# Layer 1's gate product on float16 weight parts in a diffusion transformer kernel on Trainium2

## The chip, the cores and the metric

One core of one Trainium2 chip runs the whole program in one launch. The metric is the time of one execution in microseconds on the device. A core has TensorE (PE: matrix products into PSUM; its weight loads are listed apart as PEld), VectorE (DVE), ScalarE (ACT), GpSimd (POOL) and SyncE (SP), each with its own queue of instructions that it runs in order, and 16 DMA engines that serve the queues on which transfers are issued. Here SyncE and GpSimd issue nearly all of the loads.

## The reference, cut to what matters

Two layers of a diffusion transformer on 256 tokens and 256 context rows of width 2048. Each layer modulates its normalized input with a shift, a scale and a gate that come from a product of the condition with `ada_w`; layer 0 mixes with a Fourier branch, layer 1 with windowed attention, and both multiply the branch's output by `silu(z)`, where z is a part of the product of h with the layer's input weights.

```python
def _attention_branch(h, hc, w_in, sink, rows, cols, need_ctx):
    ...
    q, k, v, z = jnp.split(h @ w_in, [D_BRANCH, D_BRANCH + kvw, D_BRANCH + 2 * kvw], axis=-1)
    ...
    y = jnp.moveaxis(o, 0, 1).reshape(b, n, D_BRANCH) * jax.nn.silu(z)
...
def reference(x, c, ctx, c_ctx, norm_g, ada_w, ada_b, w_out, ...):
    for i in range(DEPTH):
        ...
        shift, scale, gate = jnp.split((jax.nn.silu(c) @ ada_w[i] + ada_b[i])[:, None, :], 3, axis=-1)
        h = _rmsnorm(x, norm_g[i]) * (1 + scale) + shift
        ...
        x = x + gate * (y @ w_out[i])
    return _rmsnorm(x, final_g)
```

In layer 1, z has 4096 columns for the 256 tokens only, so its weights are 2048 x 4096 float32, 32 MB.

## The kernel before, in words

**Accuracy by parts.** A float32 operand is kept as a high and a low part, and a product is the sum of three products (high by high, high by low, low by high): `mm3`, lines 145 to 147. Two kinds of parts occur. In the float32 kind (`half_split`, lines 66 and 67) ScalarE rounds 1024 columns of a weight tile to the high part `wh`, and VectorE subtracts to get the low part `wl`. In the float16 kind (`split16`, lines 137 and 138) both parts `wf` are float16, and the weights are first multiplied by a power of two `up` that keeps them in float16's span. That power comes from the sum of the squares of all the weights, so those must have been read once before; the inverse power is multiplied in later. Layer 0's gate product and output product are of the float16 kind.

**The stages that the change touches** follow each other in time:

- *Output product of layer 0* (658 to about 1002 us): 32 steps `i`, in two halves of 16; a step takes one 1 MB weight tile `wo0` through SyncE's queue into one of three `raw` buffers (line 50), splits it into two `wf` in one of six `ws` buffers each, and does 48 products of 512 columns. Beside it run three other loads of work. `scan_loads` (line 824, GpSimd's queue) brings pieces of 512 columns of weights that are needed later, and `scan_sums` (line 817) squares and sums them on ScalarE a step later; this goes on for steps 0 to 13 only. `xT`, the layer's input, is loaded on GpSimd's queue in steps 12 to 15 and 28 to 31. And jobs of `ada_jobs` bring the modulation's weights `adw` of layer 0's gate and of layer 1: a job is one tile of 2048 columns, and its dot products with the condition's row `cb` run on VectorE (line 796; one or two per half of 1024 columns). `ada_rate` says how many jobs a step has, where nothing is listed one. Ahead of this stage such a job comes as two halves, `zr` on SyncE's queue (two buffers) and `wa` on GpSimd's (from the six `ws` buffers); within the stage it comes whole on SyncE's queue into a `raw` buffer (`out0[0]` is true there).
- *Transition* (to about 1004 us): row sums and the normalization of layer 1's input.
- *Key stage* (about 1004 to 1092 us): the modulated rows are made as float32 parts, for the tokens `h1` (tiles `hx1`; named h in the profile) and for the context `h1c`, and the key and value product runs over eight tiles `wkv`, split by lines 66 and 67. Then PSUM is emptied by ScalarE (`S.copy` and `Abs`, lines 1135, 1136 and 1142), a product sums the absolute values for the scale of v (line 1147), and attention begins.
- *Attention* (1092 to about 1632 us): a list of units (`units`) is emitted between the stages of softmax, two units to a stage (`filler`): 64 units of the q product (float32 parts), 32 blocks of the z product with two units each, and 12 units `o` of the output product. A z unit (lines 1320 to 1326) does for each of eight ranks k of 128 rows one product of `wh` with the whole 512-column tile `hx1[k]`, high and low part of h side by side, and one of `wl` with its first 256 columns. After the block's second unit the two halves of PSUM are added (lines 1330 and 1331), then comes z's tanh (1332) and its product (1333). `stage_s` makes scores, softmax and its float16 parts `f` (lines 1377 and 1378), which SyncE turns by DMA into `ft`; `stage_o` (lines 1395 and 1396) multiplies them with v in float16 products of 256 columns. `d_turn` (line 1209) prepares `dsc`, the factor that undoes the scale of v when the branch's output is multiplied by z's part.

The order of the instructions on each engine is made by a scheduler from the order in which they are written; `tc.issue_after(x)` ties what is written under it behind x.

Of the kernel before, what the change touches and what calls it, by code (L numbers as in the profile page):

```python
# [10 lines left out]
F32 = mybir.dt.float32  # L11
# [6 lines left out]
P = 128  # L18
# [14 lines left out]
def tile_dit(ctx: ExitStack, tc: tile.TileContext, a: dict, out: bass.AP):  # L33
# [591 lines left out]
    def h_bound():  # L625
        m = adap.tile([P, 2], F32, name="hm")
        V.tensor_reduce(m[:, 0:1], gs0.rearrange("p k s -> p (k s)"), axis=AX.X, op=ALU.max, apply_absolute_value=True)
        V.tensor_reduce(m[:, 1:2], sh0.rearrange("p k s -> p (k s)"), axis=AX.X, op=ALU.max, apply_absolute_value=True)
        V.scalar_tensor_tensor(m[:, 0:1], m[:, 0:1], 46.0, m[:, 1:2], op0=ALU.mult, op1=ALU.add)
        return as_b(m[:, 0:1])  # L630
# [8 lines left out]
    for g in range(G):  # L639
# [6 lines left out]
        if g == 13:  # L646
            with tc.issue_after(evacs[g - 2][1]), tc.issue_after(evacs[g - 2][0]):
                hb = h_bound()
                n4 = as_b(nrm[:, 30:38])
# [119 lines left out]
    def ada_jobs():  # L769
        for pieces in ((0,), (1, 2, 3)):  # L770
            for kh in range(2):
# [9 lines left out]
                if True:  # L781
                    for i, fg in order:
                        for f in range(2):
                            q = slice(f * 1024, f * 1024 + 1024)
                            if f == 0 and not out0[0]:
                                wf = adat.tile([P, 1024], F32, tag="zr", name="zr", bufs=2)
                                nc.sync.dma_start(wf, a["adw"][i, kh, fg][:, q])
                            elif not out0[0]:
                                wf = wsp.tile([P, 1024], F32, tag="ws", name="wa")
                                nc.gpsimd.dma_start(wf, a["adw"][i, kh, fg][:, q])  # L790
                            else:
                                if f == 0:
                                    w = raw(a["adw"][i, kh, fg])
                                wf = w[:, q]
# [17 lines left out]
    scans, pend = iter(range(64)), []  # L812

    def scan_sums():
        while pend:
            t, j = pend.pop(0)
            S.activation(t, t, AF.Square, accum_out=scn[:, j : j + 1])

    def scan_loads(n):
        for j in [next(scans) for _ in range(n)]:  # L820
            for q in range(2):
# [3 lines left out]
                pend.append((t, j * 2 + q - 64 * (j >= 40)))  # L825
# [20 lines left out]
    with tc.tile_pool(name="yp", reuse_waits="tile", bufs=32) as ypool:  # L846
# [142 lines left out]
        ada_rate = {**{i: 2 for i in (*range(6, 10), *range(17, 25))}, **{i: 0 for i in (14, 15, 16, 29, 30, 31)}}  # L989
        for i in range(32):  # L990
# [5 lines left out]
            if sw == 0:  # L996
                with tc.issue_after(last_cast[0]):
                    scan_sums()
                scan_loads({6: 1, 7: 1, 8: 1, 9: 1}.get(i, 2) if i < 14 else 0)
# [8 lines left out]
            elif i == 31:  # L1008
# [24 lines left out]

    x1d = dram.tile([2, P, D], F32, name="x1d")
# [57 lines left out]
    with tc.tile_pool(name="h1", reuse_waits="tile", bufs=16) as h1p:  # L1092
# [4 lines left out]
        with tc.tile_pool(name="kvp", reuse_waits="tile", bufs=2) as kvp:  # L1097
            hc1 = []
            oner = kvp.tile([P, P], F32R, name="oner", bufs=1)
            S.activation(oner, ident, AF.Identity, bias=1.0, scale=0.0)  # L1100
            for k in range(KT):
# [16 lines left out]
                hc1.append(hc)  # L1118
            o = [[psum() for _ in range(2)] for _ in range(4)]
            for kg in range(8):  # L1120
                with tc.issue_after(h_end[0]), tc.issue_after(sq_end[0]):
                    w = ws_split(raw(a["wkv"][kg])) if kg else [w0, half_split(wr, 1)]
                for j in range(2):
                    k = kg * 2 + j
                    wh, wl = w[j]
                    for tb in range(4):
                        h = (hx1, hc1)[tb // 2][k]
                        c = (tb % 2) * P
                        for kv in range(2):
                            q = slice(kv * 512, (kv + 1) * 512)  # L1130
                            mm3(o[tb][kv], h[:, c : c + P], h[:, N + c : N + c + P], wh[:, q], wl[:, q], k == 0, k == KT - 1)
            kr = []
# [36 lines left out]
        with tc.tile_pool(name="at", reuse_waits="tile", bufs=2) as at:  # L1169
# [35 lines left out]
            def d_turn(half):  # L1205
# [3 lines left out]
                V.tensor_copy(dsc[:, half * 4 : half * 4 + 4], o[:, 0::P])  # L1209
# [65 lines left out]
            def prep(u):  # L1275
# [6 lines left out]
                return half_split(raws1[src], i % 2)  # L1282

            ready = {}

            def emit_unit():
# [30 lines left out]
                else:  # L1317
                    if i == 0:
                        o.append(psum())
                    for k in range(i * 8, i * 8 + 8):  # L1320
                        q = slice((k % 8) * P, (k % 8 + 1) * P)
                        for part in (0, 1) if k < KT - 1 else (1, 0):
                            if part == 0:
                                PE.matmul(o[0], wh[:, q], hx1[k], start=k == 0, stop=k == KT - 1)  # L1324
                            else:
                                PE.matmul(o[0][:, 0:N], wl[:, q], hx1[k][:, 0:N], start=False, stop=False)  # L1326
                    if i == 1:
                        th = at.tile([P, N], F32, tag="th", name="th", bufs=3)
                        zs = at.tile([P, N], F32, tag="zs", name="zs", bufs=1)
                        S.copy(zs, o[0][:, N : 2 * N])  # L1330
                        V.tensor_tensor(zs, o[0][:, 0:N], zs, op=ALU.add)
                        S.activation(th, zs, AF.Tanh, scale=0.5)
                        V.scalar_tensor_tensor(th, th, 1.0, zs, op0=ALU.add, op1=ALU.mult)
# [326 lines left out]
```

## Time and profile before

| | us |
|---|---|
| three runs | 1776.87, 1776.41, 1772.83 |
| median | 1776.41 |
| profiled execution, its time | 1775.4 |
| its span, first to last instruction | 1773.6 |

The profile is of one execution. Its page gives for each engine the busy time, the share of the span and the number of instructions (26403 in all). The chain that ended last is followed back from the last instruction. A group of instructions is one line of the program on one engine with its tiles (output<-inputs) and shapes; behind the count stand the busy time in us, the mean of one in ns, and the idle time of the engine just before them with what ended it. A row of DMA issues has the tile, the queue, the count, the size and the median time from issue to landing in us.

### The profile page before, as it was taken

To read this page: it belongs to the slowest core of one execution; us is meant where nothing else is said; L and a number is where in the kernel's file an instruction comes from. 1 tells how busy PE (TensorE), PEld (TensorE's weight loads), DVE (VectorE), ACT (ScalarE), POOL (GpSimd) and SP (SyncE) were. 2 spreads that over 40 slices of the span, in tenths; PEclk is the share of its full clock that TensorE was granted. 3 is DMA by queue.
4 is the path that set the end of the run, shared out by engine and by line. 5 is a ranking of instruction groups with operands and counts; after the bars stand their busy time and mean duration, and the time that the engine had idled before them with its cause. 6 is when DMAs were issued, how large, how long until landed. Compare 5 with 4: busy or idle time off the path is not lost.

```text
span 1773.6 us, 26403 instructions
## 1 busy us (share of the span) xinstructions
PE 1738.5 (98%) x9517; PEld 1221.7 (69%) x9517; DVE 1393.7 (79%) x2401; ACT 1060.4 (60%) x1989; POOL 294.8 (17%) x368
## 2 busy tenths in 40 slices
PE   6999999999999999999999999999999999999997
PEld 4679999644444444446444888788888888887886
DVE  5779888797777788876885744899999999996455
ACT  5545556477777745553122534787888888885343
POOL 0002111212222132000000000412302230233010
PEclk9999999999999999999999999999999999999999
DMA  9998999778998889865775323588888888887543
GB/s 393 417 346 252 282 264 262 291 285 318 329 306 316 314 293 349 324 249 181 288 297 187 120 95 119 166 207 200 223 205 211 214 214 211 208 212 248 191 166 143
DMA packets 220962, 438.74 MB, mean 247 GB/s; under 512 B 154720, under 2 KB 155120, under 8 KB 189088
## 3 DMA queue, kind: packets, MB, share of 16 engines
q1 hardware_dynamic: 182784, 351.85, 60.6%
q0 software_dynamic: 33904, 78.25, 14.8%
q10 hardware_dynamic: 4144, 6.95, 1.2%
q8 instruction: 75, 1.23, 0.3%
q14 instruction: 55, 0.45, 0.1%
HBM read 391.91 MB, written 12.59 MB: 228 GB/s over the span
## 4 chain that ended last, share of the span: by engine, by line
PE 90%; DVE 4%; DMA 3%; ACT 2%; issue 1%; POOL 0%; ACTq 0%; POOLq 0%; SPq 0%; DVEq 0%
PE ps L145 24%; PE ps L147 24%; PE ps L146 24%; PE ps L1324 6%; PE ps L1326 3%; PE ps L1395 1%; PE ps L1360 1%; PE ps L1361 1%; PE ps L1396 1%; DMA ft<-f 1%; PE ps L286 1%; DMA raw<-in_awp 1%; DVE wl L67 1%; ACT act L864 0%; ACT wf L137 0%
## 5 line engine op out<-in xcount | busy, mean ns | idle before, releaser
L67 DVE TENSOR_TENSOR wl<-raw,wh 128x1024 fp32r<-128x1024 f32 x213 | 281.1, 1324 | 145.5 <-ACT wh L66 129.2
L66 ACT CAST wh<-raw 128x1024 fp32r<-128x1024 f32 x213 | 222.4, 1045 | 178.4 <-PE ps L146 149.7
L146 PE MATMUL ps<-act,wf 128*128 128x512 f16 x512 | 194.0, 379 | 0.0
L147 PE MATMUL ps<-act,wf 128*128 128x512 f16 x512 | 191.1, 379 | 0.0
L145 PE MATMUL ps<-act,wf 128*128 128x512 f16 x512 | 189.8, 379 | 0.6 <-ACT wf L137 0.3
L1324 PE MATMUL ps<-h,wh 128*128 128x512 f32 x512 | 184.8, 396 | 0.0
L147 PEld LDWEIGHTS <-wf 128*128 128x128 f16 x960 | 93.9, 98 | 113.3
L145 PEld LDWEIGHTS <-wf 128*128 128x128 f16 x960 | 93.7, 98 | 113.4 <-ACT wf L137 4.3
L145 PE MATMUL ps<-y,wf 128*128 128x512 f16 x448 | 169.5, 379 | 0.9 <-ACT wf L137 0.9
L146 PE MATMUL ps<-y,wf 128*128 128x512 f16 x448 | 169.8, 379 | 0.0
L146 PEld LDWEIGHTS <-wf 128*128 128x128 f16 x960 | 93.9, 98 | 109.0
L147 PE MATMUL ps<-y,wf 128*128 128x512 f16 x448 | 165.6, 379 | 0.0
L137 ACT ACTIVATE wf<-raw,nrm 128x1024 f16<-128x1024 f32 x56 | 61.2, 1140 | 153.2 <-DMA raw<-in_wo 131.4
L1326 PE MATMUL ps<-h,wl 128*128 128x256 f32 x512 | 138.6, 281 | 0.0
L146 PE MATMUL ps<-wl,h 128*128 128x512 f32 x320 | 126.7, 396 | 0.0
L147 PE MATMUL ps<-wh,h 128*128 128x512 f32 x320 | 125.3, 395 | 0.0
L145 PE MATMUL ps<-wh,h 128*128 128x512 f32 x320 | 124.0, 402 | 0.0
L1378 DVE SCALAR_TENSOR_TENSOR f<-p,sm,f 128x512 f16<-128x512 f32 x128 | 107.4, 859 | 8.6 <-ACT f L1377 8.3
L138 DVE SCALAR_TENSOR_TENSOR wf<-raw,tn,wf 128x1024 f16<-128x1024 f32 x64 | 79.8, 1282 | 42.6 <-ACT wf L137 42.6
L1365 ACT ACTIVATE p<-ps,mx 128x512 f32<-128x512 f32 x128 | 87.9, 688 | 37.2 <-DVE mx L1362 30.8
L1324 PEld LDWEIGHTS ps<-h,wh 128*128 128x128 f32 x512 | 96.2, 188 | 18.9
L1377 ACT ACTIVATE f<-p,sm 128x512 f16<-128x512 f32 x128 | 87.6, 717 | 31.6 <-DMA ft<-f 12.5
(394 smaller groups left out, 4450.2 us busy)
## 6 DMA issues: line engine op xcount, KB each, us to landing
raw<-in_wz SPq DMA_DIRECT2D x64, 1024.0 KB, 5.5
raw<-in_adw SPq DMA_DIRECT2D x38, 1024.0 KB, 6.0
raw<-in_awp SPq DMA_DIRECT2D x32, 1024.0 KB, 13.1
act<-in_wo POOLq DMA_DIRECT2D x128, 256.0 KB, 7.4
raw<-in_wo SPq DMA_DIRECT2D x32, 1024.0 KB, 6.6
raw<-in_wq SPq DMA_DIRECT2D x32, 1024.0 KB, 5.1
raw<-in_wu SPq DMA_DIRECT2D x32, 1016.0 KB, 6.9
raw<-in_wo1b SPq DMA_DIRECT2D x16, 1024.0 KB, 4.9
```

Of the source, the lines that this page charges most:

```text
L66: last_cast[0] = S.copy(h, src).ins
L67: last_sub[0] = eng.tensor_tensor(l, src, h.bitcast(F32), op=ALU.subtract).ins
L137: last_cast[0] = S.activation(w[:, 0], src, AF.Copy, scale=up).ins
L138: last_sub[0] = V.scalar_tensor_tensor(w[:, 1], src, up, w[:, 0], op0=ALU.mult, op1=ALU.subtract).ins
L145: PE.matmul(o, wh, xh, start=start, stop=False)
L146: PE.matmul(o, wh, xl, start=False, stop=False)
L147: return PE.matmul(o, wl, xh, start=False, stop=stop).ins
L1324: PE.matmul(o[0], wh[:, q], hx1[k], start=k == 0, stop=k == KT - 1)
L1326: PE.matmul(o[0][:, 0:N], wl[:, q], hx1[k][:, 0:N], start=False, stop=False)
L1365: S.activation(pt[tb], so[tb], AF.Exp, bias=mx[:, tb : tb + 1], scale=-1.0, accum_out=sm[:, tb : tb + 1])
L1377: S.activation(f[:, 0:512], pt[tb], AF.Copy, scale=sm[:, tb : tb + 1])
L1378: V.scalar_tensor_tensor(f[:, 512:1024], pt[tb], sm[:, tb : tb + 1], f[:, 0:512], op0=ALU.mult, op1=ALU.subtract)
```

## The change

1. **z in float16 parts.** A unit of z takes `wf` parts (`split16` with the power `upz`) and does three products of 256 columns per rank (`mm3`) with new float16 parts `hz` of the tokens' rows. The tanh and the product behind it read PSUM directly, with the inverse scale `hdn`, and the copy and addition `zs` go. `dsc` gets the inverse power `dnz`. The split of a z weight is tied behind the softmax's split of the third last stage.
2. **The squares of z's weights ahead of time.** All 32 MB are read once more, in 64 half tiles of 1024 columns: 25 in the output stage (`scan_loads1`, two pieces of 512 columns each, per step by `w_rate`), squared on ScalarE as before, and 39 in the key stage (`loads2`, four buffers `pz`, GpSimd's queue), squared by `sums2` on ScalarE (28) and VectorE (11).
3. **The scales.** `h_bound` of layer 1's scale and shift in step 28, sent through memory to all partitions; `h_up` in the key stage; 16 `make_hz` (two VectorE instructions and one of ScalarE each, 256 columns wide); `z_scale` after unit 1 of attention, with three products of one column.
4. **The modulation's weights** come as half tiles `zr` and `wa` in the output stage as well. `ada_rate` of step 25 is 2 (was 1) and of step 28 is 0 (was 1).

```diff
@@ ada_jobs @@
-                            if f == 0 and not out0[0]:
+                            if f == 0:
                                 wf = adat.tile([P, 1024], F32, tag="zr", name="zr", bufs=2)
                                 nc.sync.dma_start(wf, a["adw"][i, kh, fg][:, q])
-                            elif not out0[0]:
+                            else:
                                 wf = wsp.tile([P, 1024], F32, tag="ws", name="wa")
                                 nc.gpsimd.dma_start(wf, a["adw"][i, kh, fg][:, q])
-                            else:
-                                if f == 0:
-                                    w = raw(a["adw"][i, kh, fg])
-                                wf = w[:, q]
@@ output stage @@
-        ada_rate = {**{i: 2 for i in (*range(6, 10), *range(17, 25))}, **{i: 0 for i in (14, 15, 16, 29, 30, 31)}}
+        ada_rate = {**{i: 2 for i in (*range(6, 10), *range(17, 26))}, **{i: 0 for i in (14, 15, 16, 28, 29, 30, 31)}}
+        w_rate = {**{i: 1 for i in (10, 14, *range(17, 26), 30)}, **{i: 2 for i in (15, 16, 26, 27, 29)}, 28: 3}
...
-            if sw == 0:
-                with tc.issue_after(last_cast[0]):
-                    scan_sums()
-                scan_loads({6: 1, 7: 1, 8: 1, 9: 1}.get(i, 2) if i < 14 else 0)
+            with tc.issue_after(last_cast[0]):
+                scan_sums()
+            if i < 14:
+                scan_loads({6: 1, 7: 1, 8: 1, 9: 1}.get(i, 2))
+            scan_loads1(w_rate.get(i, 0))
@@ key stage @@
+            def sums2(act_only=False):
+                for n in range(len(pend)):
+                    t, c = pend.pop(0)
+                    if n % 5 < 3 or act_only:
+                        S.activation(t, t, AF.Square, accum_out=c)
+                    else:
+                        V.tensor_tensor_reduce(t, t, t, 1.0, 0.0, ALU.mult, ALU.add, c)
+
+            def loads2(n):
+                for j in [next(scans1) for _ in range(n)]:
+                    t = kvp.tile([P, 1024], F32, tag="pz", name="pz", bufs=4)
+                    nc.gpsimd.dma_start(t, a["wz1"][j // 2][:, j % 2 * 1024 : j % 2 * 1024 + 1024])
+                    pend.append((t, scn[:, j - 25 : j - 24]))
+
+            def make_hz(k):
...
+                V.scalar_tensor_tensor(t, x1[k][:, 0:N], gsz[:, k : k + 1], r_bc1[:, 0:N], op0=ALU.mult, op1=ALU.mult)
+                S.activation(h[:, 0:N], t, AF.Identity, bias=shz[:, k : k + 1])
+                V.scalar_tensor_tensor(h[:, N : 2 * N], t, shz[:, k : k + 1], h[:, 0:N], op0=ALU.add, op1=ALU.subtract)
...
+                with tc.issue_after(last_cast[0]), tc.issue_after(ends[min(kg * 4 + 3, 15)][0]):
+                    sums2(kg < 3)
...
+                with tc.issue_after(pow_end[0]):
+                    loads2((5, 5, 5, 5, 5, 5, 5, 4)[kg])
@@ attention @@
-                return half_split(raws1[src], i % 2)
+                if kind == "q":
+                    return half_split(raws1[src], i % 2)
+                with ExitStack() as ties:
+                    for ins in f_ends[-3] if len(f_ends) > 2 else ():
+                        ties.enter_context(tc.issue_after(ins))
+                    return split16(raws1[src], i % 2, upz)
...
-                        for part in (0, 1) if k < KT - 1 else (1, 0):
-                            if part == 0:
-                                PE.matmul(o[0], wh[:, q], hx1[k], start=k == 0, stop=k == KT - 1)
-                            else:
-                                PE.matmul(o[0][:, 0:N], wl[:, q], hx1[k][:, 0:N], start=False, stop=False)
+                        mm3(o[0][:, 0:N], wh[:, q], wl[:, q], hz[k][:, 0:N], hz[k][:, N : 2 * N], k == 0, k == KT - 1)
...
-                        zs = at.tile([P, N], F32, tag="zs", name="zs", bufs=1)
-                        S.copy(zs, o[0][:, N : 2 * N])
-                        V.tensor_tensor(zs, o[0][:, 0:N], zs, op=ALU.add)
-                        S.activation(th, zs, AF.Tanh, scale=0.5)
-                        V.scalar_tensor_tensor(th, th, 1.0, zs, op0=ALU.add, op1=ALU.mult)
+                        S.activation(th, o[0][:, 0:N], AF.Tanh, scale=hdn)
+                        V.scalar_tensor_tensor(th, th, 1.0, o[0][:, 0:N], op0=ALU.add, op1=ALU.mult)
```

How instructions stand on three engines, before and after. First TensorE within a unit of z in attention; before, with the h tiles numbered:

```order
L1324 MATMUL ps<-h_9841,wh 128x512
L1326 MATMUL ps<-h_9841,wl 128x256
L1324 MATMUL ps<-h_9850,wh 128x512
L1326 MATMUL ps<-h_9850,wl 128x256
L1324 MATMUL ps<-h_9859,wh 128x512
L1326 MATMUL ps<-h_9859,wl 128x256
```

The same place after, one rank:

```order
L145 LDWEIGHTS wf
L145 MATMUL ps<-hz,wf 128x256
L146 LDWEIGHTS wf
L146 MATMUL ps<-hz,wf 128x256
L147 LDWEIGHTS wf
L147 MATMUL ps<-hz,wf 128x256
```

Two products of 512 and 256 columns for a rank have become three of 256.

Second, ScalarE at the end of the key stage, before: the casts of the last key weights (from the second `h1c` on only casts stand there), then the copies that empty PSUM (lines 1135, 1136 and 1142).

```order
L1108 ACTIVATE h1c<-ht,sh_85 128x256
L66 CAST wh<-raw 128x1024 x9
L1135 COPY act<-ps 128x512
L1136 ACTIVATE act<-ps 128x512
L1135 COPY act<-ps 128x512
```

After, the same place (lines 1208, 1209 and 1215 are the same copies; line 1160 is a square of `sums2`):

```order
L1176 ACTIVATE hz<-ht,adab 128x256 x2
L1160 ACTIVATE pz,scn<-pz 128x1024
L66 CAST wh<-raw 128x1024
L1160 ACTIVATE pz,scn<-pz 128x1024
L66 CAST wh<-raw 128x1024
L1160 ACTIVATE pz,scn<-pz 128x1024 x2
L66 CAST wh<-raw 128x1024
L1160 ACTIVATE pz,scn<-pz 128x1024
L1208 COPY act<-ps 128x512
L1209 ACTIVATE act<-ps 128x512
```

Squares now stand between the casts, and the last of them right ahead of the copies; a few more follow the first copies.

Third, SyncE's queue late in the output stage, before:

```order
L50 DMA raw<-in_adw 128x2048
L50 DMA raw<-in_wo 128x2048
L50 DMA raw<-in_adw 128x2048
L50 DMA raw<-in_wo 128x2048 x3
L50 DMA raw<-in_wkv 128x2048 x3
L1043 DMA x1d<-act 128x512 x8
```

And after:

```order
L787 DMA zr<-in_adw 128x1024 x2
L50 DMA raw<-in_wo 128x2048
L787 DMA zr<-in_adw 128x1024 x2
L50 DMA raw<-in_wo 128x2048
L50 DMA raw<-in_wkv 128x2048 x3
L1063 DMA x1d<-act 128x512 x8
```

The whole tiles in the `raw` buffers have become first halves in `zr`; the loads of `wo` have the three `raw` buffers to themselves and are issued further ahead of the half tiles, which then stand last in the queue.

89 lines of the change are left out of this document (75 added, 14 removed).

## The prediction

> **What bounds the kernel now.** I read the busy times first, then the chain of work that ended last, then what TensorE waits for, and then a table of stretches, because each stage has its own limit.
>
> ```profile
> PE 1738.5 (98%) x9517; PEld 1221.7 (69%) x9517; DVE 1393.7 (79%) x2401; ACT 1060.4 (60%) x1989; POOL 294.8 (17%) x368
> PE 90%; DVE 4%; DMA 3%; ACT 2%; issue 1%; POOL 0%; ACTq 0%; POOLq 0%; SPq 0%; DVEq 0%
> ...
> PE ps L145 <- DVE dh L254: 13.3, 2, 12.0
> ...
> PE ps L145 <- ACT wf L137: 1.2, 3, 0.9
> ```
>
> TensorE is busy for 98% of the span and carries 90% of the chain. Its two longest waits on one line are 13.3 us, at a place that the change leaves alone, and split weights have kept it waiting 1.2 us in all. So time is won where TensorE has less to do, and lost where the work added elsewhere makes it wait. The table below cuts the touched stages: columns are start:end, length, busy time and instructions of TensorE, of its weight loads, of VectorE, ScalarE and GpSimd, then TensorE's clock, the DMA engines' busy share and what they moved.
>
> ```profile
> core 0: us, PE busy (x) PEld busy (x) DVE busy (x) ACT busy (x) POOL busy (x), PEclk, DMA share, GB/s
> 658.00:735.00 77.00, 77.00 (x359) 34.89 (x358) 65.70 (x95) 43.97 (x89) 15.04 (x28) 1.00 0.94 341
> ...
> 826.00:900.00 74.00, 73.40 (x341) 33.28 (x342) 66.22 (x100) 17.84 (x18) 1.26 (x3) 1.00 0.74 283
> 900.00:972.00 72.00, 72.00 (x335) 32.86 (x334) 51.71 (x78) 18.82 (x20) 1.07 (x2) 1.00 0.66 241
> ...
> 1004.00:1050.00 46.00, 46.00 (x198) 37.03 (x198) 34.71 (x69) 22.11 (x40) 0.00 (x0) 1.00 0.38 129
> 1050.00:1092.00 42.00, 42.00 (x181) 33.81 (x180) 12.10 (x15) 10.93 (x14) 0.00 (x0) 1.00 0.27 94
> ...
> 1520.00:1568.00 48.00, 48.00 (x290) 41.54 (x289) 46.00 (x91) 41.83 (x89) 5.04 (x6) 1.00 0.89 207
> ```
>
> The first three stretches are the output product of layer 0 (658 to about 1002 us), the next two the key and value product (to 1092), the last one a piece of the attention stage (to about 1632). TensorE is full in all; the clock is 1.00. The DMA engines are nearly idle in the key stage (129 and 94 GB/s) and moved 341 GB/s at a share of 0.94 at the start of the output stage, so about 341/0.94 = 363 GB/s is what they can do with such transfers. VectorE has almost no room in attention (46.0 of 48).
>
> **A. The gate product of layer 1.** A rank of 128 input rows costs one 512-column and one 256-column float32 product now and three 256-column float16 products afterwards. TensorE's own timeline (start, duration) shows both kinds side by side.
>
> ```profile
> 1331.66 0.27 PE L1396 MATMUL ps<-ft,v 128*128 128x256 f16 x1
> ...
> 1332.31 0.27 PE L1396 MATMUL ps<-ft,v 128*128 128x256 f16 x1
> ...
> 1332.77 0.39 PE L1324 MATMUL ps<-h,wh 128*128 128x512 f32 x1
> 1333.00 0.28 PE L1326 MATMUL ps<-h,wl 128*128 128x256 f32 x1
> 1333.12 0.39 PE L1324 MATMUL ps<-h,wh 128*128 128x512 f32 x1
> ...
> 1334.51 0.39 PE L1324 MATMUL ps<-h,wh 128*128 128x512 f32 x1
> ```
>
> The durations overlap, since products are pipelined, so I use starts. From 1332.77 to 1334.51 lie five pairs: 1.74/5 = 0.348 us for a pair. From 1331.66 to 1332.31 lie six float16 products of 256 columns: 0.65/6 = 0.108 us each, 0.325 for three. There are 32 blocks of 16 ranks, 512 in all: 512 x (0.348 - 0.325) = **-11.8 us**. These products already load new weights before each one, so the three weight loads in place of two are in the 0.108. The other end: if they ran no quicker than the float32 product of the same 256 columns (1333.00 to 1333.12, 0.12 us less rounding, 0.115 from 0.348/3), 512 x (0.348 - 0.345) = -1.5 us. I take -11.8.
>
> Per block a ScalarE copy and a VectorE addition go too:
>
> ```profile
> L1331 DVE TENSOR_TENSOR zs<-ps,zs 128x256 f32<-128x256 f32 x32 | 13.2, 414 | 0.0
> L1330 ACT COPY zs<-ps 128x256 f32<-128x256 f32 x32 | 11.9, 372 | 0.7
> ```
>
> They lie beside TensorE and count nothing in the sum. But TensorE gets 16 x 0.0233 = 0.37 us quicker per block and VectorE loses 0.41 us, so VectorE's share of 46.0 of 48 does not rise, and TensorE remains the bound there. The DMA share goes from 0.89 to about 0.94 if the stage is 5% shorter per block (7.4 to 7.0 us). The added tie of the weights' split behind the softmax's split (three score stages earlier) orders VectorE's queue; behind it stand only the splits of the next unit, and I price it at 0, with rival 3 as its other end.
>
> **B. The output stage.** 25 half loads (13.1 MB) of the gate weights are squared there as 50 pieces, and the modulation's weights come as half tiles. The rows of the parts:
>
> ```profile
> L817 ACT ACTIVATE act<-act 128x512 f32<-128x512 f32 x128 | 78.6, 615 | 0.0
> L817 ACT ACTIVATION_READ_ACCUMULATOR act<-act 128x1 f32 x128 | 24.0, 188 | 0.0
> L824 POOL DMA_DIRECT2D act<-in_wo x128 | 68.3, 538 | 44.7 <-ACT act L817 26.6 <-PE ps L147 4.8 <-issue 2.5
> L138 DVE SCALAR_TENSOR_TENSOR wf<-raw,nrm,wf 128x1024 f16<-128x1024 f32 x56 | 69.9, 1279 | 19.3 <-ACT wf L137 19.0
> L796 DVE CUSTOM_DVE_ANT_0 junk<-raw,cb 128x1024 f32<-128x1024 f32 x44 | 53.7, 1220 | 11.0 <-DMA raw<-in_adw 10.0 <-ACT cb L776 1.0
> L796 DVE DVE_READ_ACCUMULATOR2_ANT acc<- 128x1 f32 x224 | 18.3, 82 | 0.0
> ...
> act<-in_wo POOLq DMA_DIRECT2D x128, 256.0 KB, 7.4
> zr<-in_adw SPq DMA_DIRECT2D x26, 512.0 KB, 6.8
> wa<-in_adw POOLq DMA_DIRECT2D x26, 512.0 KB, 5.3
> act<-in_xT POOLq DMA_DIRECT2D x32, 256.0 KB, 8.8
> raw<-in_adw SPq DMA_DIRECT2D x38, 1024.0 KB, 6.0
> raw<-in_awp SPq DMA_DIRECT2D x32, 1024.0 KB, 13.1
> ```
>
> The squares: 50 x (0.615 + 0.188) = 40 us on ScalarE, which is busy for 17.84 of 74 and 18.82 of 72 us there: covered. Their loads are issued on GpSimd, 50 x 0.54 = 27 us on an engine with 1 us of work. The DMA engines: one half load of 0.52 MB in each step of 10.35 us (48 float16 products of 512 columns at twice 0.108) is 51 GB/s, so 283 becomes 334 GB/s, 0.92 of the 363: covered, but no longer with much room.
>
> The half tiles change who can wait. Before, a whole tile came into one of three buffers of 1 MB; now the first half takes one of two small buffers on SyncE's queue, and the second one of the six that the weights' parts share, on GpSimd's. In the nine steps 17 to 25, two jobs run in each, so each small buffer must turn round once in a step: landing, then at most two dot products of 1.220 + 0.082 = 1.30 us. With the 6.8 us that these same half tiles took earlier: 6.8 + 2.6 = 9.4 of 10.35. VectorE has up to 2 x 1.28 + 6 x 1.30 = 10.4 us of work in such a step (a step averages 9.3, as 66.22 of 74 says), and dot products stand in its queue ahead of the next weights' low parts, so a late half makes TensorE wait. GpSimd's queue is one too: where it waits for one of the six shared buffers, the loads of the pieces to square stand behind it, and ScalarE's square of a late piece stands ahead of the next cast. At 5.3 us of landing the cost is 0; at 8.8, 1.05 us over in each step, 9.5; at 13.1 it would be 9 x 5.35 = 48. I take **+1 us**, nearest to its own row of 6.8, for single late tiles. The bound on the largest weights (two reductions) and one job moved from step 28 to 25 fall into VectorE's free 20 us of 900 to 972: 0.
>
> [...]
>
> **C. The key stage.** The other 39 half loads (20.4 MB) are squared there, 28 on ScalarE and 11 on VectorE, from four buffers, and 16 float16 copies of h are made. The nearest rows, and ScalarE's timeline at the stage's end (start, duration, idle before):
>
> ```profile
> L645 ACT ACTIVATE pz<-pz 128x1024 f32<-128x1024 f32 x12 | 12.8, 1065 | 5.5 <-DMA pz<-in_wz 5.5
> L863 DVE SCALAR_TENSOR_TENSOR act<-act,gs,r_bc 128x256 f32<-128x256 f32 x32 | 14.0, 479 | 3.3 <-DMA act<-in_xT 3.3
> L864 ACT ACTIVATE act<-act,sh 128x256 f16<-128x256 f32 x32 | 14.5, 501 | 16.3 <-DVE act L863 16.3
> ...
> 1086.17 1.05 ACT L66 CAST wh<-raw 128x1024 fp32r<-128x1024 f32 x1 [4.55 <-PE ps L146]
> 1087.80 0.59 ACT L1135 COPY act<-ps 128x512 f32<-128x512 f32 x1 [0.58 <-PE ps L147]
> ```
>
> ScalarE: 33.0 (22.11 + 10.93) + 28 x 1.25 + 16 x 0.50 = 76 of 88 us. VectorE: 46.8 + 11 x 1.30 + 16 x 2 x 0.48 = 76.5 of 88. DMA: the 10 MB of now (129 x 46 + 94 x 42 = 9.9) and 20.4 more are 30.3 MB, 344 GB/s over 88 us, 0.95 of the 363. All three fit, none with ease. The order decides more than the sums: squares stand between the casts of the key weights and ahead of the copies that empty PSUM (1087.80), each in ScalarE's queue, so a tile that lands late holds them, then the sums for the value scale, then TensorE. The four buffers turn round 39/4, about 9 times, in what I take as 85 us (1019 to 1104), 9.7 us a round: 0.54 for the issue, the landing, 1.25 for the square. So landings up to 7.9 us cost nothing. With 5.3 a round is 7.1, with 7.4 it is 9.2, with 8.8 it is 10.6, and then 0.9 x 9 = +8. I take the row nearest in load, 7.4 at 341 GB/s, which still fits, and **+2 us** for casts that come late behind a square (the slack is the 4.55 us of idle); bounds 0 and +8.
>
> **D.** After unit 1 of attention come three one-column products and five tiny VectorE operations for the weights' scale, the first time that TensorE meets a result of the last squares. Its products are there in about 0.1 us each: **+0.5**, with the wait itself already in C.
>
> **Sum:** -11.8 + 1 + 2 + 0.5 = -8.3. Against the profiled execution's 1775.4: 1767.1; the median of the three runs is 1.0 above it, so **1768 us**. With B and C at 0 it would be 1765, with C's +8 it would be 1774, with the late half tiles of B some 1776; the likeliest case's own range is 1763 to 1771.
>
> **Rivals.**
> 1. The ring of four buffers in the key stage becomes the bound. For: 344 GB/s asked where 363 is the most seen, and ScalarE's order. Against: four loads are in flight, and 7.4 us fits. With landings of 8.7 us: 0.8 x 9 = 7 us more, 1775, no change. Chance 0.16.
> 2. The half tiles' ring in the output stage becomes the bound (the slower side): two buffers where three of twice the size stood, at 334 GB/s. It costs from 7.75 us of landing on, 9 us for each further one; from 9.3 us it is slower than now. At 9.5 to 10 us it gives 16 to 20 us, about 1784. For: rows of 8.8 and 13.1 for other loads in crowded stages. Against: the halves' own 6.8, and 5.3 on the other queue. Chance 0.21. [...]
> 3. Attention does not follow: the new products take 0.115 rather than 0.108, or VectorE's and the transposes' queue (0.94 busy) set the pace, so that nearly all of A is lost: -1.5 to -3 with 3.5 of cost, 1776. Against: 0.108 is measured between two such units. Chance 0.11.
>
> **The numbers.** Forecast 0.52, all of it faster by over 0.3% (5.3 us, about what a measurement of this kernel tells from no change). Rivals 1 and 3, 0.27 together, are within 0.3%; rival 2, 0.21, slower. Range 1762 to 1786: it takes in rivals 1 and 3 and half of 2, and leaves out some 0.15.
>
> **What would show it.** The starts of the float16 products of a gate block lie 0.108 us apart, a block 0.37 us shorter (A; 0.115 is rival 3). The stretch of the output stage keeps its length; otherwise TensorE waits for split weights and VectorE for the half tiles (rival 2). The copies after the key product begin at the same distance from the stage's start, and no square waits long for its load (else rival 1). I am wrong altogether if TensorE waits at a place that I did not name, or its clock falls under the denser float16 work.

## The result and the profile after

The changed kernel takes 1797.93 us (median of four runs, 1796.97 to 1798.26), the kernel before 1775.64 beside it: 1.0127 times as long, 95% interval 1.0109 to 1.0144. The forecast was 1768, the range ended at 1786. The profiled execution has a span of 1796.5 us, 22.9 more than before.

The table of stretches shows that the loss is not where the loads were added. First the stretches of the output and the key stage in the changed kernel, with the columns of the table in the prediction:

```profile
826.00:900.00 74.00, 74.00 (x344) 33.56 (x343) 53.97 (x78) 30.22 (x57) 26.36 (x50) 1.00 1.01 378
900.00:972.00 72.00, 72.00 (x335) 33.19 (x334) 63.95 (x101) 33.87 (x68) 11.22 (x21) 1.00 0.82 293
1004.00:1050.00 46.00, 46.00 (x199) 37.05 (x198) 39.40 (x86) 37.12 (x70) 8.45 (x16) 1.00 0.88 315
1050.00:1092.00 42.00, 42.00 (x181) 33.64 (x180) 28.18 (x50) 26.67 (x49) 8.97 (x17) 1.00 0.89 333
```

TensorE is full in all four although up to 378 GB/s are moved. The product for the value scale begins at 1090.96 us, 0.8 earlier than before (1091.80). The loss comes behind that, in two pieces: 6.7 us up to the first score and 16.4 in attention (with 0.6 in what follows, less the 0.8, that is the 22.9).

The first piece: the first score is at 1139.64, 48.7 us behind the value scale's product, where it was 42.0 (1133.78). ScalarE and VectorE in between, in the changed kernel:

```profile
1100.06 1.06 ACT L1160 ACTIVATE pz<-pz 128x1024 f32<-128x1024 f32 x1 [3.45 <-DMA pz<-in_wz]
1102.18 1.23 DVE L67 TENSOR_TENSOR wl<-raw,wh 128x1024 fp32r<-128x1024 f32 x1 [5.19 <-ACT wh L66]
```

A square of `sums2` (line 1160) waits 3.45 us for its half tile. The cast behind it in ScalarE's queue is late, VectorE waits 5.19 us for that cast, and TensorE then waits 3.7 us for VectorE (the rows `dn` and `wl` further down) and works at half its clock for 3.4 us from 1117.0 on. In run 14 below, which is the same up to there, the last wait of a square is 0.98 us, TensorE doesn't wait, and the distance is 42.4 us.

The second piece: from the first score to the last product of the softmax with v, the stretch in which every row below is taken, attention looks like this, the kernel before first:

```profile
1133.78:1613.89 480.11, 473.82 (x2612) 393.11 (x2611) 449.85 (x826) 394.76 (x782) 125.38 (x102) 1.00 0.84 211
```

And the changed kernel:

```profile
1139.64:1636.14 496.50, 470.89 (x3124) 385.43 (x3123) 446.82 (x794) 391.14 (x751) 122.42 (x102) 0.99 0.81 206
```

Attention has become 16.4 us longer instead of shorter. TensorE stands idle for 25.6 us of it (496.50 - 470.89) where it was 6.3. Its busy time fell by 2.9 only, although the products of z are nearly as quick as forecast. On TensorE's timeline of the changed kernel, the first and the last of the 24 products of a unit:

```profile
1468.59 0.28 PE L145 MATMUL ps<-hz,wf 128*128 128x256 f16 x1
...
1471.11 0.27 PE L147 MATMUL ps<-hz,wf 128*128 128x256 f16 x1
```

That is 2.52/23 = 0.1096 us each, 0.329 for three, and 512 x (0.348 - 0.329) = -9.9 us (unrounded) of term A's -11.8. VectorE shows the other side: 446.82 us of work, 3.0 less than before, and 49.7 us without work, where it had 30.3. What TensorE waited for longest, in the changed kernel (total us, times, longest):

```profile
PE ps L145 <- DVE dh L254: 12.4, 2, 11.1
PE ps L1467 <- DMA ft<-f: 12.3, 11, 2.0
PE ps L1316 <- POOL act L1110: 8.8, 6, 1.9
...
PE ps L1281 <- DVE dn L1229: 1.9, 2, 1.1
PE ps L146 <- DVE wl L67: 1.8, 2, 1.4
```

The first is far ahead of the change, and the last two belong to the first piece. The others are attention's: 12.3 us for the turned tiles of the softmax (before 3.8), and, new, 8.8 for GpSimd's rotation of the next q, which line 1316 (the transposes of q, `q_turn`) reads. VectorE's groups (after the bar: busy time, mean ns, idle time just before them and who ended it) show it waiting for ScalarE ahead of the softmax's low part. In the kernel before:

```profile
L1378 DVE SCALAR_TENSOR_TENSOR f<-p,sm,f 128x512 f16<-128x512 f32 x128 | 107.4, 859 | 8.6 <-ACT f L1377 8.3
```

In the changed kernel, with z's splits below:

```profile
L1449 DVE SCALAR_TENSOR_TENSOR f<-p,sm,f 128x512 f16<-128x512 f32 x128 | 103.8, 833 | 19.9 <-ACT f L1448 19.4
L138 DVE SCALAR_TENSOR_TENSOR wf<-raw,adab,wf 128x1024 f16<-128x1024 f32 x64 | 94.5, 1504 | 2.1 <-ACT wf L137 2.1
```

It waits 19.4 us for ScalarE's high part instead of 8.3. That wait alone is not the loss: run 7 below has 18.2 us of it, and 55.4 us of VectorE without work, and TensorE waits far less. z's splits take 1504 ns each, where the same instruction took 1279 in the row for `nrm` in the prediction, and takes 1288 in run 7. What they meet depends on where they stand. A piece of VectorE's timeline, and of GpSimd's at the same time:

```profile
1396.25 2.48 DVE L138 SCALAR_TENSOR_TENSOR wf<-raw,adab,wf 128x1024 f16<-128x1024 f32 x2
1398.64 0.15 DVE L1438 SCALAR_TENSOR_TENSOR sm<-sm,es 128x2 f32<-128x2 f32 x1
...
1403.58 3.72 DVE L138 SCALAR_TENSOR_TENSOR wf<-raw,adab,wf 128x1024 f16<-128x1024 f32 x2
1407.22 0.69 DVE L1438 SCALAR_TENSOR_TENSOR sm<-sm,es 128x2 f32<-128x2 f32 x1
```

```profile
1403.27 1.27 POOL L1104 TENSOR_TENSOR act<-act,rope 128x512 f32<-128x512 f32 x1 [24.19 <-ACT act L1303]
...
1411.39 3.47 POOL L1110 TENSOR_TENSOR act<-act,rt 128x512 f32<-128x512 f32 x2
```

In 26 of the 64 stages two splits or more now stand together between the reduction of the last score and the softmax's sum (line 1438); before it was 12, and nearly everywhere else one stood there. A pair takes 2.48 us; beside the rotation, which runs from 1403.27 to 1414.86, the pair takes 3.72 and the sum, a matter of 0.15 us, 0.69. The sum then is late, and with it ScalarE's f (at 1408.19, behind 1.61 us of idle time) and the turned tile that TensorE waits for.

Some waits cost more than themselves. TensorE's timeline behind two waits for the rotation:

```profile
1475.57 0.33 PE L1316 MATMUL ps<-ident,act 128*128 128x128 f32 x1 [0.69 <-POOL act L1110]
1477.77 0.55 PE L1316 MATMUL ps<-ident,act 128*128 128x128 f32 x3 [1.87 <-POOL act L1110]
...
1479.32 0.44 PE L145 MATMUL ps<-hz,wf 128*128 128x256 f16 x1
1479.55 0.42 PE L146 MATMUL ps<-hz,wf 128*128 128x256 f16 x1
1479.76 0.42 PE L147 MATMUL ps<-hz,wf 128*128 128x256 f16 x1
```

The products are 0.21 to 0.23 us apart, against 0.1096 in the unit above. The granted clock (third figure from the end of a row) was halved three times in this stretch, for 3.4 us twice and for 6.8 the third time (to 1639.2, past the end):

```profile
1478.80:1482.20 3.40, 3.40 (x16) 2.04 (x16) 2.56 (x8) 2.12 (x3) 0.00 (x0) 0.50 0.57 241
1543.60:1547.00 3.40, 2.93 (x10) 2.09 (x11) 2.70 (x6) 0.62 (x1) 0.42 (x1) 0.51 0.88 301
1632.40:1635.80 3.40, 2.62 (x21) 2.05 (x19) 1.11 (x2) 1.36 (x2) 0.00 (x0) 0.50 1.01 417
```

In the 3.41 us ahead of each, TensorE was busy for 1.36, 0.73 and 1.39 us; 3.41 us with 1.74 (from 1373.00) were followed by the full clock. Without any of this TensorE's busy time in attention would be 473.8 - 9.9 = 463.9 us; it is 470.9. So the 16.4 us are -9.9 for the product, +19.3 of idle time and +7.0 of longer work, the last being what is left over. Half of the 8.95 us of work in the three rows, about 4.5, went to the lower clock (before, one such time, from 1612.3, cost 0.7); the other 3 us or so are not placed. What halves the clock is not shown; ahead of the first time stand two waits of 0.69 and 1.87 us with one product of 0.33 us between them.

### The profile page after: what moved, and what is told of

Its sections match the earlier page's. It is cut to its first block, busy times and chain, and to the rows that moved or that the text cites. A ratio compares the mean times of both kernels' runs of the same rounds, so it can differ in the third digit from the quotient of the medians.

```text
span 1796.5 us, 27741 instructions
## 1 busy us (share of the span) xinstructions
PE 1738.3 (97%) x10035; PEld 1215.7 (68%) x10035; DVE 1415.6 (79%) x2442; ACT 1125.8 (63%) x2129; POOL 360.5 (20%) x497
## 3 DMA queue, kind: packets, MB, share of 16 engines
q0 software_dynamic: 49056, 131.80, 22.9%
## 5 line engine op out<-in xcount | busy, mean ns | idle before, releaser
L67 DVE TENSOR_TENSOR wl<-raw,wh 128x1024 fp32r<-128x1024 f32 x149 | 192.0, 1291 | 108.3 <-ACT wh L66 103.7
L145 PEld LDWEIGHTS <-wf 128*128 128x128 f16 x1472 | 144.1, 98 | 128.1 <-issue 9.1
L66 ACT CAST wh<-raw 128x1024 fp32r<-128x1024 f32 x149 | 155.3, 1044 | 114.8 <-PE ps L146 102.4
L147 PEld LDWEIGHTS <-wf 128*128 128x128 f16 x1472 | 144.3, 98 | 121.9 <-DVE wf L138 2.3
L146 PEld LDWEIGHTS <-wf 128*128 128x128 f16 x1472 | 144.3, 98 | 114.7
L147 PE MATMUL ps<-hz,wf 128*128 128x256 f16 x512 | 140.2, 274 | 1.6 <-DVE wf L138 1.6
L145 PE MATMUL ps<-hz,wf 128*128 128x256 f16 x512 | 140.8, 275 | 0.0
L146 PE MATMUL ps<-hz,wf 128*128 128x256 f16 x512 | 140.3, 274 | 0.0
L145 PE MATMUL ps<-wh,h 128*128 128x512 f32 x320 | 126.9, 402 | 0.0
L147 PE MATMUL ps<-wh,h 128*128 128x512 f32 x320 | 126.2, 397 | 0.0
L1449 DVE SCALAR_TENSOR_TENSOR f<-p,sm,f 128x512 f16<-128x512 f32 x128 | 103.8, 833 | 19.9 <-ACT f L1448 19.4
L827 ACT ACTIVATE act<-act 128x512 f32<-128x512 f32 x178 | 109.5, 616 | 7.0 <-DMA act<-in_wo 4.6
```

Source lines behind the costliest of these rows:

```text
L66: last_cast[0] = S.copy(h, src).ins
L67: last_sub[0] = eng.tensor_tensor(l, src, h.bitcast(F32), op=ALU.subtract).ins
L145: PE.matmul(o, wh, xh, start=start, stop=False)
L146: PE.matmul(o, wh, xl, start=False, stop=False)
L147: return PE.matmul(o, wl, xh, start=False, stop=stop).ins
L827: S.activation(t, t, AF.Square, accum_out=c)
```

## The experiments

Theory S said that attention was lost by the order of VectorE's queue, theory L that the loads and squares were the loss. All ratios are to runs of the kernel before on the same chip.

**1. z alone.** Constants in place of all that makes the scales, whole tiles for the modulation:

```diff
-                V.tensor_reduce(s, hb1, axis=AX.X, op=ALU.max)
...
+                V.memset(upz, 1024.0)
+                V.memset(hdn, 0.5 / 1024)
+                V.memset(dnz, 1.0 / 1024)
...
-            sums2()
-            zw2 = keepc[:, 7:8]
```

> Only the float16 product of z is kept; its scales are constants, so nothing is squared ahead, no bound is made, and the modulation's weights come as whole tiles as before (the result then rests on constants that fit these inputs). Theory S, the loss is in attention, where VectorE's queue now has z's two splits in front of the softmax's sums: attention stays as long as in the changed kernel, about 480 us or more from the first score to the last product, and the time is 1788 to 1796, better than the changed kernel by at most the 6 to 7 us that are lost ahead of the first score. Theory L, the loss comes from the added loads and squares: 1764 to 1768, as the sum of the prediction without terms B to D.

1791.06 us, 1.0092 (1.0070 to 1.0114). From the first score on it is as slow as the changed kernel (497.8 us); the 6.7 us ahead of the first score are gone (42.0 us from the value scale's product, as before). So attention's loss is there without any of the added loads and squares.

**2. The scales alone.** z as before, all else as changed:

```diff
-                        mm3(o[0][:, 0:N], wh[:, q], wl[:, q], hz[k][:, 0:N], hz[k][:, N : 2 * N], k == 0, k == KT - 1)
+                                PE.matmul(o[0], wh[:, q], hx1[k], start=k == 0, stop=k == KT - 1)
...
+                                PE.matmul(o[0][:, 0:N], wl[:, q], hx1[k][:, 0:N], start=False, stop=False)
```

> Everything of the change but the float16 product: all squares, the bound, the float16 rows, the scales and the half tiles are there, and z is multiplied in float32 parts as before, so that the scales are made and not used. Theory S: 1776 to 1784, that is before plus what the squares cost ahead of the first score (up to 7 us). Theory L: about 1798 + 12 = 1810, since the loads would cost 34 us and nothing is gained.

1777.10 us, 1.0017 (1.0004 to 1.0030): 3 us for 32 MB more of loads, their squares and the half tiles. Theory L is out as the main cause.

**3. No tie**, and **4. splits apart**. In place of the tie of the changed kernel none, and for run 4 a tie of the second split behind the reciprocal of the softmax's sum (`fill` is 0 in a stage's first unit, 1 in its second):

```diff
-                    for ins in f_ends[-3] if len(f_ends) > 2 else ():
-                        ties.enter_context(tc.issue_after(ins))
+                t = ([] if fill[0] == 0 else r_ends)
+                with tc.issue_after(t[-1]) if t else nullcontext():
```

> The changed kernel without the tie of z's split behind the softmax's split. The order on VectorE then has up to four of z's splits around one sum of the softmax. Theory S: the time moves with the order, 1795 to 1815, rather slower. Theory L: unchanged, 1797 to 1799.

> The changed kernel with another tie: the first split of z in a stage is free, the second is tied behind the reciprocal of the softmax's sum of the same stage, so that VectorE has one split ahead of the sum and one behind it, as the float32 splits stood before. Theory S: attention gets shorter by 10 us or more, 1778 to 1788. Theory L: unchanged, 1797 to 1799.

1801.99 (1.0160, 1.0135 to 1.0185) and 1786.50 (1.0070, 1.0051 to 1.0088). By these ratios an order alone is worth some 10 us to the better and perhaps 6 to the worse (the intervals of run 3 and of the changed kernel overlap). In run 4 VectorE has 13.4 us less of work (433.4 us), but attention still has 490.4 us, 6.1 less than in the changed kernel and not 10; most of the rest lies ahead of the first score, where the waits for loads are. And TensorE waits 7.4 us for z's low splits, where it was 1.6.

**5. No low split, 6. transposes later, 7. no rotation, 8. both repairs.** Theory G put the loss on the rotation of q on GpSimd. The edits (of run 5 without the line of the products; its splits lose the tie too):

```diff
-                with ExitStack() as ties:
...
-                    return split16(raws1[src], i % 2, upz)
+                w = wsp.tile([P, 2, 1024], F16, tag="ws", name="wf")
+                last_cast[0] = S.activation(w[:, 0], raws1[src][:, i % 2 * 1024 : i % 2 * 1024 + 1024], AF.Copy, scale=upz).ins
+                return w[:, 0], w[:, 0]
```

```diff
-                if defer and defer[0][0] + 2 < j:
+                if defer and defer[0][0] + 3 < j:
```

```diff
-                        roped(t, t0, tb, actp, "act", GP)
+                        t = t0
```

> The changed kernel with z's weights in their high part alone (the low part is left out, and the second and third product read the high part again, so TensorE has as many products as before, and VectorE has none of z's 64 splits). Theory S, VectorE's queue holds up the softmax: attention is bound by TensorE again, z stages of 7.0 us and no waits, 1762 to 1770. Theory G, the wait comes from the rotation of the next q on GpSimd, which ends late and slows VectorE beside it: the transposes of q still wait, 1785 to 1792.

> The changed kernel with the transposes of q one unit later on TensorE. Theory G: the 8.7 us of waits for GpSimd go and with them the clock's dips behind them, 1784 to 1790. Theory S: those waits turn into waits for the softmax's transposes, 1794 to 1800, unless the scheduler also changes the order on VectorE.

> The changed kernel without the rotation of q on GpSimd in the seven later head groups (left out, q goes to its transposes as copied). Instructions on VectorE stand in the same order as in the changed kernel. Theory G: no wait for GpSimd, and VectorE's splits beside it take 1.26 instead of 1.87 us: 1775 to 1782. Theory S: the waits for GpSimd go, those for the softmax's transposes stay, 1786 to 1792.

> Both repairs together, z's splits one ahead of and one behind the softmax's sum, and the transposes of q one unit later. If they add up (11 us from the first, up to 9 from the second): 1776 to 1784. If the second has nothing left to give, since the first had only one wait for GpSimd of 1.1 us: 1784 to 1788.

Run 7 is the one that counts: 1776.59 us, 1.0009 (0.9993 to 1.0024), 21 less than the changed kernel with the same order on VectorE. Its stretch of attention:

```profile
1139.73:1617.36 477.63, 466.87 (x3124) 385.56 (x3123) 422.21 (x794) 391.23 (x751) 45.96 (x46) 0.99 0.83 214
```

VectorE has 24.6 us less of busy time, for the same 794 instructions, and the stage is 18.9 shorter. ScalarE's busy time is the same (391.14 and 391.23). Run 5 gave 1785.14 (1.0066, 1.0049 to 1.0083), not the 1762 to 1770 of theory S:

```profile
1134.43:1621.61 487.18, 468.83 (x3125) 385.74 (x3123) 360.40 (x730) 391.43 (x751) 102.56 (x102) 0.99 0.83 211
```

With 86 us less of work VectorE has 127 us of idle time, and TensorE waits all the same. So the amount of VectorE's work is not by itself the bound. That the order in which its queue and ScalarE's wait for each other is the bound instead is likely, but not shown. Run 6 took the waits for GpSimd away, gave 1791.35 (1.0100, 1.0074 to 1.0125), and TensorE then waited 15.4 us for the turned tiles in attention. Run 8 gave 1792.25 (1.0106, 1.0089 to 1.0124), worse than run 4: the repairs don't add up. Each also makes the scheduler order VectorE's queue anew, so neither is tried alone.

**9 to 12: what the rotation costs, and to whom.** Run 9 is the edit of run 7 in the kernel before, run 11 in that of run 1, run 12 with that of run 5. Run 10 keeps the rotation running and reads the unrotated copy:

```diff
                         roped(t, t0, tb, actp, "act", GP)
+                        t = t0
```

> The kernel before without the rotation of q on GpSimd in the seven later head groups (left out); VectorE's order is that of before. If TensorE covers the rotation in the kernel before: 1772 to 1775, no change. If the rotation costs both kernels alike and its removal from the changed kernel says nothing about the change: about 1774 - 21 = 1753.

> The changed kernel with the rotation of q still done on GpSimd, but its result left unused (the transposes take the unrotated copy). It tells the wait for the result from the load beside VectorE. If the wait is what costs (8.7 us of TensorE's waits and what follows from them): 1776 to 1781, as without the rotation. If the load is what costs, VectorE's splits being slower beside it (1.87 instead of 1.26 us): 1789 to 1797, nearly as in the changed kernel.

> The float16 product of z alone, with constant scales and no squares, and without the rotation of q on GpSimd. If the prediction's first term is there to be had once the rotation is away: 1774 - 12 = 1762, or 1762 to 1768 with the first head group's start as long as it was. If something else in attention holds the stage up: 1774 to 1778.

> Both taken away: z's low splits on VectorE and the rotation on GpSimd (both parts left out; TensorE's work as in the changed kernel). If the two hold up the same queue, so that either alone leaves some of it: 1765 to 1772 (first term -12, scales +3). If the splits play no part once the rotation is gone: 1775 to 1778, as without the rotation alone.

Run 10 took 1796.02 us (1.0128, 1.0103 to 1.0153), like the changed kernel, with its order on VectorE and ScalarE and without any wait for the rotation's result. Its stretch of attention:

```profile
1136.07:1634.34 498.27, 473.15 (x3124) 387.27 (x3123) 446.26 (x794) 391.32 (x751) 123.29 (x102) 0.98 0.80 206
```

VectorE is as slow as in the changed kernel, and TensorE idles for 25.1 us at other places. So GpSimd's work beside VectorE costs the 20 us (498.27 us of attention here, 477.63 in run 7), not the wait for its result. Run 9 took 1770.61 (0.9982, 0.9971 to 0.9993): the kernel before pays some 3 us for the same rotation. Its stretch of attention:

```profile
1133.18:1610.54 477.36, 474.20 (x2612) 393.92 (x2611) 427.16 (x826) 398.45 (x782) 48.63 (x44) 1.00 0.84 209
```

VectorE is freed of 22.7 us here too, and the stage gets shorter by 2.8 only, since TensorE with 474 us of work was the bound. Run 11 took 1770.07 (0.9982, 0.9972 to 0.9991), and its stretch:

```profile
1133.47:1610.53 477.06, 466.40 (x3124) 385.27 (x3123) 422.30 (x794) 390.42 (x750) 45.56 (x46) 0.99 0.84 215
```

That is as long as in run 9. Even without the rotation the 9.9 us of term A are not won: TensorE idles 10.7 us instead of 3.2, and its busy time fell by 7.8 only, not 9.9. The 7.5 us of new waits take back nearly all of it; what they come from is not taken apart. Run 12 took 1780.75 (1.0033, 1.0017 to 1.0048), rather worse than run 7 and against both of its readings.

**13 to 16: latency or throughput.** The product with v comes three stages behind its scores in place of two, with room made for it (the buffers and the loop's end are left out here); run 14 has the smaller buffers alone, run 15 adds the order of run 4, run 16 is run 4 without the rotation:

```diff
-                if i >= 2:
-                    stage_o(i - 2, *pts.pop(i - 2))
+                if i >= 3:
+                    stage_o(i - 3, *pts.pop(i - 3))
```

> The changed kernel with the product of the softmax with v three stages behind its scores in place of two (one more buffer for the turned tiles and one for z's tanh, one less each for the exponentials and for f, to make room). If the latency of the softmax holds TensorE up: most of the 12 us of waits for the turned tiles go, and the clock's dips with them, 1780 to 1788. If it is the throughput of VectorE's queue beside the rotation: the waits come back at another place, 1793 to 1800.

> Control for the run before: the changed kernel with one buffer less for the exponentials and for f, at the distance of two stages. 1796 to 1802 if the buffers matter little; where it is much slower, the run with three stages is read against this one.

> Three stages of distance and z's splits one ahead of and one behind the softmax's sum. If latency and order are two causes: 1772 to 1780. If the order alone did what there was to do: 1784 to 1790.

> Splits apart and no rotation on GpSimd (left out). If the two are separate causes (11 and 21 us): 1766 to 1770. If the pair of splits costs only what it meets beside the rotation: 1774 to 1780, as without the rotation alone.

Run 13 took 1797.96 us (1.0127, 1.0100 to 1.0154), run 14 1797.48 (1.0121, 1.0094 to 1.0148). In run 13 TensorE no longer waits for the turned tiles:

```profile
PE ps L147 <- DVE wf L138: 10.3, 13, 1.5
PE ps L1316 <- POOL act L1110: 6.2, 10, 0.9
PE ps L1459 <- ACT f L1448: 4.4, 1, 4.4
PE ps L1316 <- ACT p L1436: 4.0, 4, 1.0
```

It waits for VectorE's splits and ScalarE instead, for as long (28.0 us of idle time, 27.8 in run 14). The waits moved and did not go, which speaks for the throughput of the queues behind it and against latency. Run 15 took 1818.31 (1.0243, 1.0214 to 1.0271), where TensorE waited 19.5 us for z's splits, and run 16 1784.98 (1.0060, 1.0041 to 1.0079). Its order on VectorE is nearly that of run 4, but not quite; there the rotation costs 1.5 us, no more than the noise, and in the order of the changed kernel 21. In both runs TensorE waits for z's low splits (7.4 and 8.1 us), with the rotation and without. No version beat the kernel before beyond what leaving the rotation out explains.

Runs 6, 8, 11, 12, 15 and 16 came out outside both of their expected ranges, and run 9 a little below its nearer one: what a new order does to these queues was not foreseen here either.

## Why the prediction was wrong, point by point

- **A, the product itself: right in kind, 1.9 us too large.** 0.1096 us per product against the forecast 0.108, so -9.9 us.
- **A, "TensorE remains the bound there": wrong**, and this is the step that failed. It was argued from VectorE's busy time, 46.0 of 48 us, with the addition that goes. But TensorE stood idle for 25.6 us of the stage, where it had been 6.3. VectorE's saving did not come: its busy time in the stage fell by 3.0 us and not by the 13.2 of the additions, in part since z's splits got slower in their new place (1504 ns in the mean); without the rotation it fell by 4.9 (runs 9 and 11). Runs 1, 2, 7 and 10 show the cause in place of it: the rotation of q on GpSimd slows VectorE, and in the order that the change brings TensorE waits for that. VectorE's order being the same, 18.9 us of the stage go with the rotation (run 7), and none where only its result is unused (run 10). In the kernel before VectorE is slowed as much, 22.7 us, and TensorE's work covers it (run 9). And even without the rotation the step fails: TensorE's 7.8 us less of work came back as 7.5 us of waits (run 11).
- **A, the tie "at 0": wrong.** The order of z's splits is worth some -10 (run 4) to perhaps +6 us (run 3). The prediction looked at what stands behind the tie, and not at VectorE's order in attention, where the pair of splits ahead of the sum could have been seen.
- **B and C: right in the sum, C in part by luck.** 3.5 us were forecast with D, run 2 measured 3.1 (0.7 to 5.3). The half tiles `zr` landed after 6.8 us (forecast 6.8), those of the key stage after 7.1 (7.4 taken), and the output stage kept its length, so rival 2 did not happen. But C had less room than it says: 85 us over 39/4 rounds are 8.7 us a round and not 9.7, and a landing of 7.4 makes a round of 9.2. The sign of rival 1, a square that waits long for its load, is there: ScalarE waits 12.4 us in all for half tiles in the changed kernel, and the last of these waits, 3.45 us, stands at the head of the first piece of the loss.
- **D: the products as forecast, the wait not.** From the value scale's product to the first score lie 42.0 us without the scales (before, runs 1, 9 and 11) and 42.4 where TensorE never waits there (runs 4, 5 and 14): 0.4 for a forecast of 0.5. The wait, "already in C", makes it 43.5 to 48.7 in the others, and by and large the longer, the later the last square stands that waited over 0.3 us for its load: it starts 4.2 to 4.8 us behind the value scale's product in those three runs and 9.1 in the changed kernel.
- **Rival 3 named the place**, VectorE's pace in attention, but priced it as a gain that is lost, 1776 at most. It left out that waits can exceed the gain: there was no term for VectorE's own waits, for GpSimd's work beside it, or for TensorE's clock behind a wait. With these the 19.3 us of idle time and the 7.0 of longer work would have had a place. The wait for GpSimd's rotation is at a place that the prediction did not name, which was its own sign of being wrong altogether.

What stays open: why the same rotation costs 21 us in one order of the queue, 1.5 in another and 3 in the kernel before is shown as a fact and not taken apart further; where the waits of run 11 come from; and whether some order would give the 9.9 us of term A to the whole. The sixteen kernels show only that of the orders tried none does.

## What to carry to other kernels

In a stage in which two engines are nearly full (before, TensorE with 473.8 us of work and VectorE with 449.9 in attention's 480.1), less work for one of them need not shorten it. Here 7.8 us off TensorE came back as 7.5 us of waits (run 11), and 86 us off VectorE still left TensorE idle for 18.4 us (run 5). Before such a change, add up busy time and idle time of the second engine in that very stage, look at what a third engine does beside it, and read in the new order what now stands ahead of the instruction that starts the next engine. A square that waited 3.45 us for its load held up the cast behind it in ScalarE's queue, VectorE behind that by 5.19 us and TensorE by 3.7, outside the stages in which the loads were added up. And waits of TensorE cost more than their length where its clock fell behind them: two of 0.69 and 1.87 us were followed by 3.4 us at half the clock.

## What the runs showed of the hardware

VectorE took longer for the same instructions while GpSimd rotated q, though the trace has no wait of VectorE for GpSimd in attention: a pair of splits took 3.72 us beside the rotation and 2.48 without, and VectorE's 794 instructions of attention took 446.8 us with the rotation (changed kernel) and 422.2 without (run 7). Not every line got slower: the scores' reduction (line 1433) took 750 ns with the rotation and 752 without, while the softmax's low part (line 1449) took 833 and 775 and z's splits (line 138) 1504 and 1288. What makes the difference between the lines is not shown.

TensorE's clock fell to half three times in the changed kernel's attention, each time behind 3.41 us in which TensorE had been busy for 0.73 to 1.39; behind 3.41 us with 1.74 (from 1373.00) it stayed full. The clock was at 0.50 for 3.4 us twice and for 6.8 us once, and 3.4 us at half the clock cost at most 1.7. In attention the busy time that lies over the 463.9 us of the same work is 7.0 us with three such times (changed kernel) and 3.0 with two (run 7, from 1182.0 and 1612.1).
